# A hybrid encoder layer on one core: merges behind their accumulators' last additions, earlier block sums, combinations over more blocks

## The chip, the cores and the metric

The kernel runs as one program on one core of a Trainium2 chip. The metric is the device time of one launch in microseconds. The engines are named as in the profile: PE (TensorE, matrix products), DVE (VectorE), ACT (ScalarE), POOL (GpSimd) and SP (SyncE, which here issues most transfers). Each engine works through its own list of instructions in order and waits where an instruction needs the result of another engine or of a transfer.

## The reference

One layer of a streaming encoder for 2048 prompt tokens and 32 further tokens of a running stream, all in float32, with model width 1024 and a feed-forward width of 4096:

```
n = rmsnorm(x, g_mix);  z = n @ w_in
A = sliding-window attention with sinks (8 query heads, 2 key heads, width 64)
B = gated linear attention (4 heads, keys 64 wide, values 128), chunks of 64 tokens
h = x + concat(A, rmsnorm(B) * silu(rg)) @ w_out
y = h + relu(rmsnorm(h, g_ffn) @ w_up)^2 @ w_down
```

Beside y it returns the keys and values of the window and the state of the linear attention. The part that takes most of the time is the last line.

## The kernel before

A float32 product is done as three passes: each operand is split into a high part (rounded, a copy on ACT) and a low part (the rest, a subtraction on POOL or DVE), and PE sums high x high, high x low and low x high. `split_weight` and `weights` (the subtraction stands at L281 and L1454) do this for the weights, `load_tok` (L1578) for the tokens.

The program has four phases. Attention comes first, then linear attention (its decays E are formed on POOL at L946 and L954, and on DVE), then the output projection with the residual and the second norm (`op_phase`), then the feed-forward part.

**The feed-forward part** multiplies by Strassen's scheme in Winograd's form: seven products instead of eight. The tokens are in three environments, worked on in the order 1, 2, 0 with 356, 356 and 328 columns for a quarter. Each goes through 16 blocks of the feed-forward width (`NF`). A block has seven products with w_up (U) and seven with w_down (D); PE takes in turn the i-th of D for one block and the i-th of U for the block behind it, also across the border between environments. A product has twelve matmuls in two halves for each of two row groups, and for D each half has one PSUM tile of its own (`two`). DVE adds it from there to accumulators in SBUF, named P with the numbers 1 to 7 (L1580). At the end of an environment accumulators are added to one another on POOL (`merge`, L1679), and 2 to 5 are sent out (`store`, L1681). Merges with 7 and 1 are made in the last block but one. In the last block, product 1 is added to 6 and 2, and 5 and 7 to two accumulators each, so that only the merges of 6 into 3, 5 and 4 are left there.

**Weights.** The combinations of w_down's four quarters (S1 to S4) are formed ahead by `block_sums` (L723), four subtractions or additions on POOL for each part of a block, and stored in DRAM as `sd`: the first four blocks (EARLY) during attention, six more (MIDDLE) during linear attention, through one single buffer, the rest in the output projection. `down_sums` (L732) paces them: it runs beside the main text of a phase and yields numbers, which count PE time of the program's own running account until it is resumed: 6000 after a load, 3500 after each addition, 6000 after a store. In the first environment the split weights are also saved to DRAM (`save`, L1440) and read back by the others; those of the last block are made early by `keep_down`, one for each of blocks 2 to 8. `combine` (L1694) forms the token combinations of the last environment from quarters in DRAM: 8 pieces with four steps each (load, two subtractions, two more, store), one step with each product of D in blocks 9 to 13.

**The output projection** handles groups of columns; for a group it loads the residual (`load_y`, tile y), multiplies eight row pieces (PE, tile op), adds y on DVE (L1336), squares on ACT and accumulates on DVE (L1339); PE turns these into row sums (`oprb<-ones,acc`).

**What sets the order.** The text is run once by Python, and a scheduler sets each engine's list by its own running account of when operands will be ready and memory is free; loads on SP stand in the order in which it gets to them. An extra dependency without waiting (`after`) only orders two instructions. Memory that the sums' buffer takes in linear attention is used again by tiles of the projection, y among them.

Of the kernel before, what the change touches and what calls it, by code (L numbers as in the profile page):

```python
# [9 lines left out]
F32 = mybir.dt.float32  # L10
# [53 lines left out]
class Builder:  # L64
# [203 lines left out]
    def split_weight(self, src, hi, lo, hi_eng="act", lo_eng="pool", parts=1, after=None):  # L268
# [3 lines left out]
        for i in range(parts):  # L272
            ks = slice(i * k // parts, (i + 1) * k // parts)
            raw = tile_[:, ks]
            self.last_load = self.Q.dma_start(raw, src[:, ks]).ins
            if hi_eng == "act":
                self.after(self.S.activation(hi[:, ks], raw, AF.Copy), after)
            else:
                self.V.tensor_copy(hi[:, ks], raw)
            eng = self.G if lo_eng == "pool" else self.V  # L280
            eng.tensor_tensor(out=lo[:, ks], in0=raw, in1=hi[:, ks].bitcast(F32), op=ALU.subtract)  # L281

# [22 lines left out]
    def attention_phase(self):  # L305
# [3 lines left out]
        with ExitStack() as ctx:  # L309
# [337 lines left out]
            for i, t in enumerate(order):  # L647
# [13 lines left out]
                if i == 4:  # L661
                    early = [(b, c0, P) for b in range(EARLY) for c0 in range(0, 512, P)]
                    one = lambda name: self.mid.tile([P, 576], F32, tag="cc", name=name)
                    for j in range(2):
                        self.spawn(self.down_sums(early[j::2], one, 1, 3500), 13000 * j)
                if t == nt - 1:
# [64 lines left out]

    def down_sums(self, units, tile_, parts, step):  # L732

        for b, c0, n in units:
            raw = tile_(f"sd{b}_{c0}")[:, : 4 * n].rearrange("p (k m n) -> p k m n", k=2, m=2)
            self.load_block(raw, b, c0, n)
            yield 6000
            for _ in self.block_sums(raw, parts):
                yield step
            self.G.dma_start(self.sd[b][:, :, c0 : c0 + n], raw.rearrange("p k m n -> p (k m) n"))  # L740
            yield 6000

# [67 lines left out]
    def gla_phase(self):  # L810
        tc, a, V, S, G, Q = self.tc, self.a, self.V, self.S, self.G, self.Q
        nt = self.nt
        with ExitStack() as ctx:
# [274 lines left out]
            whole = lambda name: sums.tile([P, 2048], F32, tag="sd", name=name)  # L1088
            self.spawn(self.down_sums([(b, 0, 512) for b in range(EARLY, EARLY + MIDDLE)], whole, 2, 3500), 4000)
            for _ in gates(0):  # L1090
# [15 lines left out]
    def load_wout(self, pi, halves, engs):  # L1106
        w_out = self.a["w_out"].rearrange("(k p) n -> p k n", p=P)
        return [sum((self.wide_pairs(w_out, 512 * fh, f"wo{fh}", engs[j], (j,)) for j in range(2)), []) for fh in halves]

# [251 lines left out]
    def ffn_phase(self):  # L1361
# [4 lines left out]
        with ExitStack() as ctx:  # L1366
# [68 lines left out]

            products = lambda b: [DOWN[i] for i in (0, 4, 2, 1, 3, 5, 6)] if b == NF - 1 else DOWN
            kept, unsaved = self.kept, []

            def save():

                while unsaved:
                    key, t = unsaved.pop(0)
                    Q.dma_start(kept[key], f32(t))
# [86 lines left out]
            def down_weights(n, b, out):  # L1530
# [4 lines left out]
                for i, (x, _, _) in enumerate(products(b)):  # L1535
# [10 lines left out]
                    eng = V if n == 0 and i in (0, 5) and b < NF - 2 else G  # L1546
                    save()
                    out[x] = weights(f"d{b}{x}", None if made else src[x], g == 0, eng)
                    yield
                save()  # L1550

# [142 lines left out]
            def combine(step):  # L1694

                i = step % 4
                k, half = divmod(step // 4, 2)
                if k == H:
                    return
# [33 lines left out]
            for x, g, i in steps:  # L1733
# [6 lines left out]
                else:  # L1740
# [3 lines left out]
                    residual(g, i)  # L1744
                    if n == 0 and 2 <= b < 9 and i == 3:
                        keep_down(NF - 1, b - 2)
                    if n == 0 and 2 <= b < 9 and i == 5:
                        save()
                    if n == 0 and 9 <= b < 14:
                        combine(7 * (b - 9) + i)  # L1750
                    if b == NF - 2:
                        for q, x in {2: ((3, 5),), 3: ((5, 7), (4, 7)), 4: ((6, 1), (2, 1))}.get(i, ()):
                            merge(e, q, x)
                    if b == NF - 1 and i == 1:
                        for q in (3, 5, 4):
                            merge(e, q, 6)
                    if b == NF - 1 and i >= 3:
                        store(e, (3, 5, 2, 4)[i - 3], 1 + end)
                prepare()
# [142 lines left out]
```

## Time and profile before

| | us |
|---|---|
| three runs | 2267.05, 2274.03, 2277.59 (median 2274.03) |
| profiled execution | 2263.1, its span 2261.2 |
| PE busy in the span | 2142.3 (95%) |
| POOL busy | 1555.5 (69%) |
| DVE busy | 1545.1 (68%) |
| ACT busy | 1211.9 (54%) |

The span is what the hardware profiler saw of one execution, from the first to the last instruction; the execution's own time is 1.9 us longer. The median of the three runs is 10.9 us above that execution. Attention lasts until about 372 us, linear attention until about 715, the projection until about 903, and the feed-forward part until the end; the D products of its three environments end near 1390, 1848 and 2255. An idle stretch is given ahead of the instruction that ended it, with what released it; the row `<-issue` names nothing that the profile shows.

### The profile page before, as it was taken

Reading aid. Unit: us, or ns where it says so; the run is one execution under the profiler, and the core shown is the slowest. Engines: PE = TensorE matmul, PEld = TensorE weight load, DVE = VectorE, ACT = ScalarE, POOL = GpSimd, SP = SyncE. Lnnn points to the kernel's source line nnn. Section 1 sums busy time; section 2 is a strip of 40 time slices with the busy share of each in tenths; the row PEclk is TensorE's granted clock in tenths of the full one; section 3 lists DMA queues with packets and bytes.
Section 4 is the critical chain, followed back from the end, with each engine's and each line's share of the span. In section 5 each row is a group of like instructions: output and inputs, shape, how many; then the busy total and the mean of one; then the engine's idle time right before and its main releaser. Section 6 shows DMA issues by size and latency. Waiting matters only on the chain. (4 is left out here: it accounts for less than half of the span.)

```text
span 2261.2 us, 40634 instructions
## 1 busy us (share of the span) xinstructions
PE 2142.3 (95%) x14790; PEld 2010.9 (89%) x14790; DVE 1545.1 (68%) x3402; ACT 1211.9 (54%) x2692; POOL 1555.5 (69%) x1447
## 2 busy tenths in 40 slices
PE   7999999999987899999999997999999979999997
PEld 6777777888876899999999997999999979999996
DVE  7766766788993544677777764666666646766676
ACT  4555555656553122666665554566656636666662
POOL 4354555444446477778889896788877968888885
PEclk9999999999999899999999998999999989999998
DMA  7444564334345887644455575344444654444433
GB/s 249 149 154 135 199 211 141 136 110 157 101 158 180 337 332 289 232 148 156 163 180 179 164 274 180 125 139 136 136 138 130 246 198 138 143 154 143 152 112 113
DMA packets 191355, 391.00 MB, mean 173 GB/s; under 512 B 32417, under 2 KB 117586, under 8 KB 184242
## 3 DMA queue, kind: packets, MB, share of 16 engines
q1 hardware_dynamic: 157330, 331.36, 44.3%
q10 hardware_dynamic: 27120, 27.64, 3.5%
q0 software_dynamic: 6704, 29.40, 3.4%
q8 instruction: 117, 1.92, 0.3%
q14 instruction: 84, 0.69, 0.1%
HBM read 288.96 MB, written 99.38 MB: 172 GB/s over the span
## 5 line engine op out<-in xcount | busy, mean ns | idle before, releaser
L1580 DVE TENSOR_TENSOR P<-P,dn 128x712 f32<-128x712 f32 (+1 forms) x648 | 564.0, 875 | 271.2 <-PE dn L167 230.5
L44 ACT ACTIVATE u<-u 128x356 f32<-128x356 f32 (+1 forms) x384 | 174.2, 454 | 45.3 <-DVE u L1580 24.2
L44 ACT ACTIVATE r<-u 128x356 f32<-128x356 f32 (+1 forms) x192 | 88.5, 461 | 178.8 <-PE u L167 178.6
L1580 DVE TENSOR_TENSOR u<-u,r 128x356 f32<-128x356 f32 (+1 forms) x144 | 75.6, 525 | 105.9 <-PE u L167 88.0
L954 POOL TENSOR_TENSOR E<-cc 128x256 f32<-128x256 f32 (+1 forms) x117 | 68.5, 618 | 101.4 <-DVE cc L806 39.3
L1478 POOL TENSOR_TENSOR stage<-stage 128x512 f32<-128x512 f32 x90 | 116.6, 1295 | 16.5 <-DMA stage<-in_w_up 12.5
L723 POOL TENSOR_TENSOR sd<-sd 128x128 f32<-128x128 f32 (+2 forms) x136 | 101.0, 747 | 26.1 <-DMA sd<-in_w_down 21.6
L1030 DVE COPY_PREDICATED AT<-masks,A 64x64 f32<-64x64 int32 (+1 forms) x330 | 82.9, 253 | 23.0 <-ACT AT L44 12.3
L1580 DVE TENSOR_TENSOR uT<-u,uT 128x356 fp32r<-128x356 f32 (+1 forms) x192 | 94.2, 511 | 5.2 <-ACT uT L44 5.0
L1580 DVE TENSOR_TENSOR uB<-u,uB 128x356 fp32r<-128x356 f32 (+1 forms) x144 | 73.9, 513 | 26.3 <-ACT u L44 25.9
L44 ACT ACTIVATE uT<-u 128x356 fp32r<-128x356 f32 (+1 forms) x192 | 83.5, 457 | 7.7 <-DVE u L1580 7.1
L1336 DVE TENSOR_TENSOR y<-op,y 128x356 f32<-128x356 f32 (+1 forms) x48 | 23.9, 517 | 88.8 <-PE op L167 58.2
L1679 POOL TENSOR_TENSOR P<-P,P 128x712 f32<-128x712 f32 (+1 forms) x48 | 79.1, 1676 | 6.7 <-DVE P L1580 6.7
L44 ACT ACTIVATE P<-S,negm 128x192 f32<-128x192 f32 (+2 forms) x128 | 51.5, 417 | 45.1 <-DVE negm L588 31.1
L44 ACT ACTIVATE op<-y 128x356 f32<-128x356 f32 (+1 forms) x42 | 19.2, 467 | 93.0 <-DVE y L1336 89.3
L44 ACT ACTIVATE E<-E 128x1024 f32<-128x1024 f32 (+2 forms) x68 | 67.2, 1012 | 1.1
L44 ACT ACTIVATE uB<-u 128x356 fp32r<-128x356 f32 (+1 forms) x144 | 65.9, 457 | 3.0
L606 POOL TENSOR_TENSOR P<-P,es 128x512 f32<-128x512 f32 x15 | 15.5, 1034 | 68.8 <-ACT sq L44 27.1
L1580 DVE TENSOR_TENSOR u<-u,f 128x356 f32<-128x356 f32 (+1 forms) x96 | 49.9, 519 | 9.3 <-ACT u L44 9.3
L965 DVE TENSOR_TENSOR E<-E,kq 128x256 f32<-128x256 f32 (+1 forms) x117 | 54.2, 516 | 1.1 <-ACT E L44 1.0
L44 ACT ACTIVATE v<-go 128x256 f32<-128x256 f32 (+1 forms) x34 | 12.7, 379 | 75.5 <-DVE Sp L1062 39.4
L44 ACT ACTIVATE pS<-pT 128x256 f32<-128x256 f32 (+1 forms) x62 | 27.2, 491 | 43.2 <-PE pT L171 43.2
(1576 smaller groups left out, 8132.8 us busy)
## 6 DMA issues: line engine op xcount, KB each, us to landing
stage<-in_w_up SPq DMA_DIRECT2D x90, 512.0 KB, 4.0
stage<-sd SPq DMA_DIRECT2D x86, 512.0 KB, 4.7
stage<-in_w_down SPq DMA_DIRECT2D x43, 512.0 KB, 3.3
stage<-su SPq DMA_DIRECT2D x30, 512.0 KB, 4.1
sd<-sd POOLq DMA_DIRECT2D x12, 1024.0 KB, 5.5
stage<-in_w_down SPq DMA_DIRECT2D x46, 256.0 KB, 3.1
xT1a<-in_xT_prompt SPq DMA_DIRECT2D x16, 512.0 KB, 4.7
stage<-in_w_in SPq DMA_DIRECT2D x16, 512.0 KB, 5.5
```

What stands on the lines that cost most here:

```text
L44: ins = f(*args, **kw)
L606: (G if ch == 0 else V).tensor_tensor(out=dst, in0=src, in1=rb, op=ALU.mult)
L723: self.after(self.G.tensor_tensor(out=o, in0=x, in1=y, op=op), self.last_pe)
L954: G.tensor_tensor(out=e4, in0=c4, in1=ref, op=ALU.subtract)
L965: V.tensor_tensor(out=e4, in0=e4, in1=halves_of(kq, L, m), op=ALU.mult)
L1030: V.copy_predicated(dst, mk.unsqueeze(1).broadcast_to([L // nh, 2, w // m, m]), src[r].rearrange("s p (n m) -> s p n m", m=m),)
L1336: V.tensor_tensor(out=y[:, f], in0=ps, in1=y[:, f], op=ALU.add)
L1478: tt = lambda o, x, y, op: G.tensor_tensor(out=o, in0=x, in1=y, op=op)
L1580: add = lambda out, x, y, op=ALU.add: V.tensor_tensor(out=out, in0=x, in1=y, op=op)
L1679: G.tensor_tensor(out=e.acc[q][:, j : j + 2], in0=e.acc[q][:, j : j + 2], in1=e.acc[x][:, j : j + 2], op=ALU.add)
```

## The change

It has six parts.

1. `down_sums` takes its pauses as an argument. For EARLY nothing changes (3500 and 6000); for MIDDLE the step is 2200 and the pause 4000.
2. `split_weight` remembers its low part's instruction, and `load_wout` orders the high copies of the first output half's second part behind it.
3. The last block's D products run in the order 1, 6, 5, 3, 7, 4, 2; the last two were 2, 4.
4. The merges of 6 into 3, 5 and 4 were all given with product 6; now each is given with the product that adds last to that accumulator, and its store follows.
5. `save` may leave some weights unsaved for now: in the first environment saves lag two behind; in later blocks it isn't called here.
6. `keep_down` moves from blocks 2 to 8 to 7 to 13; `combine` takes four steps of every ten products, from block 2 to 13.

```diff
 def down_sums(self, units, tile_, parts, step, pause):
...
-            yield 6000
+            yield pause
...
-            self.spawn(self.down_sums([(b, 0, 512) for b in range(EARLY, EARLY + MIDDLE)], whole, 2, 3500), 4000)
+            self.spawn(self.down_sums([(b, 0, 512) for b in range(EARLY, EARLY + MIDDLE)], whole, 2, 2200, 4000), 4000)
...
-        return [sum((self.wide_pairs(w_out, 512 * fh, f"wo{fh}", engs[j], (j,)) for j in range(2)), []) for fh in halves]
+        part = lambda fh, j: self.wide_pairs(w_out, 512 * fh, f"wo{fh}", engs[j], (j,), self.last_low if j and not fh else None)
+        return [part(fh, 0) + part(fh, 1) for fh in halves]
...
-            products = lambda b: [DOWN[i] for i in (0, 4, 2, 1, 3, 5, 6)] if b == NF - 1 else DOWN
+            products = lambda b: [DOWN[i] for i in (0, 4, 2, 1, 3, 6, 5)] if b == NF - 1 else DOWN
...
-            def save():
+            def save(lag=0):
-                while unsaved:
+                while len(unsaved) > lag:
                     key, t = unsaved.pop(0)
...
-                    save()
+                    if g < 2:
+                        save(2 - 2 * g)
                     out[x] = weights(f"d{b}{x}", None if made else src[x], g == 0, eng)
                     yield
-                save()
...
-                i = step % 4
-                k, half = divmod(step // 4, 2)
-                if k == H:
+                i = step % 10
+                k, half = divmod(step // 10, 2)
+                if k >= H or i > 3:
                     return
...
-                    if n == 0 and 2 <= b < 9 and i == 3:
-                        keep_down(NF - 1, b - 2)
-                    if n == 0 and 2 <= b < 9 and i == 5:
+                    if n == 0 and 7 <= b < 14 and i == 3:
+                        keep_down(NF - 1, b - 7)
+                    if n == 0 and 7 <= b < 14 and i == 5:
                         save()
-                    if n == 0 and 9 <= b < 14:
-                        combine(7 * (b - 9) + i)
+                    if n == 0 and 2 <= b < 14:
+                        combine(7 * (b - 2) + i)
...
-                    if b == NF - 1 and i == 1:
-                        for q in (3, 5, 4):
+                    if b == NF - 1 and i >= 3:
+                        q = (3, 5, 4, 2)[i - 3]
+                        if q != 2:
                             merge(e, q, 6)
-                    if b == NF - 1 and i >= 3:
-                        store(e, (3, 5, 2, 4)[i - 3], 1 + end)
+                        store(e, q, 1 + end)
```

Two places show how instructions move. First SP, at the border of linear attention and the projection. `y00` and `y01` are the residuals of the first two groups, `u0raw` weights of the first U products, `mx0l` the third group's tokens, `sd10` a block to be summed. Before:

```order
L60 DMA u0raw_9185<-in_w_up 128x4x256 x2
L60 DMA mx0l_9162<-mix10_169 128x2848
L60 DMA ku0A11_9247<-u0A11_9244 128x1024
L60 DMA ku0A12_9251<-u0A12_9248 128x1024
L60 DMA sd10_9241<-in_w_down 128x1024 x2
L60 DMA y00_9180<-in_x_group0 128x2624
L60 DMA y01_9194<-in_x_group1 128x2624
```

And with the change:

```order
L60 DMA y00_9180<-in_x_group0 128x2624
L60 DMA u0raw_9185<-in_w_up 128x4x256 x2
L60 DMA y01_9194<-in_x_group1 128x2624
L60 DMA ku0A11_9247<-u0A11_9244 128x1024
L60 DMA ku0A12_9251<-u0A12_9248 128x1024
L60 DMA mx0l_9162<-mix10_169 128x2848
L60 DMA sd10_9241<-in_w_down 128x1024 x2
```

The first residual went from behind six loads and saves to the front, directly behind the last store of linear attention's state (`out_s_prompt`); the third group's tokens went behind the second residual and two saves.

Second POOL, at the end of the first environment. T4l is the low part of a token combination of the next environment, `stage` and `wf_u1...` its weights' combinations and splits for block 1, P3 to P6 the accumulators. Before:

```order
L1478 TENSOR_TENSOR stage_16139<-stage_16139,stage_16141 128x4x128
L1578 TENSOR_TENSOR T4l_10760<-T4l_10760,T4h_10759 128x712 x2
L1679 TENSOR_TENSOR P3_10749<-P3_10749,P6_10771 128x712
L1679 TENSOR_TENSOR P5_10750<-P5_10750,P6_10771 128x712
L1679 TENSOR_TENSOR P4_10773<-P4_10773,P6_10771 128x712
L1679 TENSOR_TENSOR P3_10749<-P3_10749,P6_10771 128x712
L1679 TENSOR_TENSOR P5_10750<-P5_10750,P6_10771 128x712
L1679 TENSOR_TENSOR P4_10773<-P4_10773,P6_10771 128x712
L1454 TENSOR_TENSOR wf_u1A11_15858<-stage_15854,wf_u1A11_15858 128x512
L1454 TENSOR_TENSOR wf_u1A12_15906<-stage_15856,wf_u1A12_15906 128x512
```

And with the change, whose lines are one further on here:

```order
L1479 TENSOR_TENSOR stage_16139<-stage_16139,stage_16141 128x4x128
L1579 TENSOR_TENSOR T4l_10760<-T4l_10760,T4h_10759 128x712 x2
L1680 TENSOR_TENSOR P3_10749<-P3_10749,P6_10771 128x712 x2
L1455 TENSOR_TENSOR wf_u1A11_15856<-stage_15852,wf_u1A11_15856 128x512
L1680 TENSOR_TENSOR P5_10750<-P5_10750,P6_10771 128x712 x2
L1455 TENSOR_TENSOR wf_u1A12_15906<-stage_15854,wf_u1A12_15906 128x512
L1680 TENSOR_TENSOR P4_10773<-P4_10773,P6_10771 128x712 x2
L1455 TENSOR_TENSOR wf_u1S2_15948<-stage_15904,wf_u1S2_15948 128x512
```

The six merges stood in one piece; they stand now in pairs, one accumulator at a time, with a split of a weight behind each pair.

More of the change, by code (lines that the diff above doesn't have):

```diff
@@ L280, in split_weight @@
             eng = self.G if lo_eng == "pool" else self.V
-            eng.tensor_tensor(out=lo[:, ks], in0=raw, in1=hi[:, ks].bitcast(F32), op=ALU.subtract)
+            self.last_low = eng.tensor_tensor(out=lo[:, ks], in0=raw, in1=hi[:, ks].bitcast(F32), op=ALU.subtract)
     def cols_pair(self, w, c0, name, engs=(("act", "pool"), ("act", "pool")), k0=0, nk=KB, after=None):
@@ L664, in attention_phase @@
                     for j in range(2):
-                        self.spawn(self.down_sums(early[j::2], one, 1, 3500), 13000 * j)
+                        self.spawn(self.down_sums(early[j::2], one, 1, 3500, 6000), 13000 * j)
                 if t == nt - 1:
@@ L730, in load_block, with down_sums @@
             self.after((queue or self.G).dma_start(raw[:, k], w[b, :, k, :, c0 : c0 + n]), self.last_pe)
-    def down_sums(self, units, tile_, parts, step):
+    def down_sums(self, units, tile_, parts, step, pause):
         for b, c0, n in units:
@@ L740, in down_sums @@
             self.G.dma_start(self.sd[b][:, :, c0 : c0 + n], raw.rearrange("p k m n -> p (k m) n"))
-            yield 6000
+            yield pause
     def prepare_gla(self, part):
```

## Prediction

> **What bounds the kernel now.** I read the header of the page first, then windows of 60 us, then every idle stretch of TensorE, and for the long ones the rows of the engines that released them.
>
> ```profile
> span 2261.2 us, 40634 instructions
> PE 2142.3 (95%) x14790; PEld 2010.9 (89%) x14790; DVE 1545.1 (68%) x3402; ACT 1211.9 (54%) x2692; POOL 1555.5 (69%) x1447
> PE   7999999999987899999999997999999979999997
> POOL 4354555444446477778889896788877968888885
> 720.00:780.00 60.00, 36.40 (x235) 36.13 (x234) 25.17 (x56) 10.90 (x24) 29.31 (x25) 0.80 0.85 314
> 780.00:840.00 60.00, 60.00 (x377) 60.00 (x376) 28.24 (x73) 12.13 (x22) 42.22 (x37) 1.00 0.88 338
> 1320.00:1380.00 60.00, 42.91 (x229) 41.65 (x228) 27.19 (x39) 22.93 (x45) 54.49 (x35) 0.83 0.66 239
> 1800.00:1860.00 60.00, 42.54 (x240) 41.32 (x240) 31.41 (x48) 21.51 (x48) 41.98 (x28) 0.83 0.67 235
> ```
>
> The columns of a window are its length, the busy time of PE, weight loads, DVE, ACT and POOL, then PE's clock, DMA's share and GB/s. TensorE is the bound: 2142.3 of 2261.2 us busy, and most windows, like 780 to 840, have no idle at all. Since no matmul is removed, the most that any change of order could win is what PE does not use: 118.9 us of idle, plus the time in which its clock was low. The idle is not spread out: three dips in the PE row of slices (one at the output projection, two at the ends of the first and second environment) hold 23.6 + 17.1 + 17.5 us, and the shares of POOL peak just before two of them.
>
> ```profile
> 745.37 1.27 PE L167 MATMUL oprb<-ones,acc 128*82 128x1 f32 x8 [23.60 <-DVE acc L1339]
> 1214.06 3.66 PE L167 MATMUL dn<-uT,wf_d10S 128*128 128x356 f32 x12 [3.12 <-DVE P L1580]
> 1369.71 2.12 PE L167 MATMUL dn<-uB,wf_d15S 128*128 128x356 f32 x6 [10.72 <-issue]
> 1374.72 2.12 PE L167 MATMUL dn<-uB,wf_d15S 128*128 128x356 f32 x6 [2.88 <-DVE P L1580]
> 1828.18 2.12 PE L167 MATMUL dn<-uB,wf_d15S 128*128 128x356 f32 x6 [10.88 <-issue]
> 1833.19 2.12 PE L167 MATMUL dn<-uB,wf_d15S 128*128 128x356 f32 x6 [2.89 <-DVE P L1580]
> 2240.49 1.33 PE L167 MATMUL dn<-uB,wf_d15S 128*128 128x328 f32 x6 [1.79 <-issue]
> 2245.13 1.98 PE L167 MATMUL dn<-uB,wf_d15S 128*128 128x328 f32 x6 [3.31 <-DVE P L1580]
> ```
>
> A row gives start, duration, the work, and in brackets how long the engine was idle ahead of it and for whom. These eight rows are the places that the change can reach; I take them in turn.
>
> **Output projection: the residual's load moves ahead.** The 23.60 us are a chain across four engines:
>
> ```profile
> 695.02 0.47 SPq L60 DMA_DIRECT2D out_s_prompt<-Sp  x1
> 719.93 0.58 POOL L740 DMA_DIRECT2D sd<-sd  x1
> 726.48 0.80 SPq L60 DMA_DIRECT2D y<-in_x_group  x2
> 732.60 3.38 DVE L1336 TENSOR_TENSOR y<-op,y 128x328 f32<-128x328 f32 x8 [29.77 <-DMA y<-in_x_group]
> 738.03 7.29 DVE L1339 TENSOR_TENSOR acc<-acc,op 128x328 f32<-128x328 f32 x7
> 714.29 0.42 PE L167 MATMUL op<-m1h,wo00h 128*128 128x328 f32 x1 [0.53 <-ACT op L44]
> y<-in_x_group SPq DMA_DIRECT2D x2, 1312.0 KB, 8.1
> 738.00:741.00 3.00, 0.00 (x0) 0.00 (x0) 2.86 (x6) 1.74 (x5) 1.74 (x2) 0.50 1.01 418
> ```
>
> POOL sends the last of the MIDDLE sums away at 719.93; only then is the space free into which SP loads the residual (726.48); it lands, DVE adds (732.60), accumulates (738.03), and PE can form the row sums at 745.37. The change's denser steps (2200 for 3500, pauses of 4000 for 6000) put that last store ahead of the last pieces of E, and SP's load right behind `out_s_prompt`, with no engine left to wait for. So it can be issued at about 695.5 and has landed by 695.5 + 8.1 = 703.6, before the products it is added to: those are all there when PE turns to the second half (714.29). DVE's eight additions and accumulations (3.38 + 7.29 for seven, so about 12 us) then run beside the products instead of behind them; the last sum comes some 2 to 3 us after 714.3 (an estimate: one of each, and ACT's square between), and PE, which reaches the row sums at 745.37 − 23.60 = 721.77, finds them there. The ceiling is 23.6 us and, by the clock of 0.50 in the last row, 1 more for the start behind it. The lower bound is DMA's: it is 0.85 and 0.88 busy in the two windows of this stage, so what PE no longer waits for may wait for transfers instead. The window with the stall moved 314 GB/s x 60 us = 18.8 MB; at the 338 of the next window that takes 55.7 us, a gain of 4.3. Against this, DMA reached 418 within the stall itself (738 to 741). Nearest is the ceiling, less a little for loads that come later: I take **22** (4 to 24.6).
>
> **Ends of the first two environments: merges behind the last additions.** Before, POOL adds acc6 into 3, 5 and 4 in one piece, ahead of the DVE additions to these:
>
> ```profile
> 1361.29 3.31 POOL L1578 TENSOR_TENSOR T4l<-T4l,T4h 128x712 fp32r<-128x712 f32 x2
> 1364.57 9.92 POOL L1679 TENSOR_TENSOR P<-P,P 128x712 f32<-128x712 f32 x6
> 1367.91 1.70 DVE L1580 TENSOR_TENSOR P<-P,dn 128x712 f32<-128x712 f32 x2 [9.89 <-POOL P L1679]
> 1374.00:1377.00 3.00, 2.28 (x8) 2.31 (x9) 0.70 (x2) 0.00 (x0) 0.49 (x1) 0.50 0.00 0
> 1379.09 2.11 PE L167 MATMUL dn<-uT,wf_d15S 128*128 128x356 f32 x12
> 1835.00:1838.00 3.00, 3.00 (x13) 3.00 (x12) 0.90 (x1) 0.00 (x0) 0.00 (x0) 0.50 0.53 155
> ```
>
> DVE stands 9.89 us for POOL; with one PSUM tile for each half, PE stands behind DVE: 10.72 us, and 2.88 once more two additions later. The change makes each merge follow its accumulator's last addition, so no addition waits for POOL. What goes: 10.72 + 2.88 = 13.6 at the first end and 10.88 + 2.89 = 13.8 at the second. To this comes the low clock: at 0.50 half of a busy time is lost, so 1.06 of the six matmuls' 2.12 at 1369.71, and 1.14 of the 2.28 busy in the window from 1374; at the second end 1.06 twice, and 1.50 of the 3.00 from 1835. Ceilings: 13.6 + 2.2 = 15.8 and 13.8 + 3.6 = 17.4. The six merges of 1.65 us are still to be done, between the splits of the next environment's weights. They may come from 1364.6 on, and the first split behind them is wanted when the three pairs of products that are left are through, some 12 us later (an estimate: six products of about 2.1 us, as at 1379.09); two merges (3.3) ahead of each split leave it room. SP's stores of the results wait for the merges, and loads queue behind them, but those are for later blocks. I take **15.5** (8 to 15.8) and **17** (9 to 17.4), the lower ends for half being given back to such a queue. The merges of block 14, ahead of these, stay where they were.
>
> **The last end.** Here the same six merges end the program:
>
> ```profile
> 2235.64 9.26 POOL L1679 TENSOR_TENSOR P<-P,P 128x656 f32<-128x656 f32 x6 [6.75 <-DVE P L1580]
> 2255.05 0.84 DVE L1580 TENSOR_TENSOR P<-P,dn 128x656 f32<-128x656 f32 x1 [0.35 <-PE dn L167]
> 2257.75 0.47 SPq L60 DMA_DIRECT2D out_yT_sample<-P  x1
> ```
>
> The waits of 1.79 and 3.31 us go, and the six matmuls behind the second need not take 1.98 (1.33 behind the first): 5.8. DVE is then the next limit (0.84 an addition, two to a product), so not all of it comes. The last accumulator, 2, needs no merge, and that of 4 (2 x 1.55) fits beside its additions; a merge that came last would cost 1.6 of the gain. I take **5.5** (3 to 5.8).
>
> **Middle of the first environment: combinations over twelve blocks, kept weights in 7 to 13.** The removed crowd is blocks 9 to 13:
>
> ```profile
> 1206.21 6.55 DVE L1454 TENSOR_TENSOR wf_d10A<-stage,wf_d10A 128x512 fp32r<-128x512 f32 x1
> L1454 DVE TENSOR_TENSOR wf_d10A<-stage,wf_d10A x2: 885/3716/6548, 1186.2 to 1206.2; 128x512 fp32r<-128x512 f32 x2
> L1454 DVE TENSOR_TENSOR wf_d4A<-stage,wf_d4A x2: 684/685/686, 1022.7 to 1039.6; 128x512 fp32r<-128x512 f32 x2
> 1165.00:1190.00 25.00, 24.38 (x150) 24.09 (x150) 18.61 (x28) 16.45 (x35) 23.08 (x22) 1.00 0.57 177
> L1710 POOL TENSOR_TENSOR quads<-quads x32: 487/566/1026, 1166.4 to 1272.6; 128x178 f32<-128x178 f32 x32
> ```
>
> The same split takes 0.685 us on DVE in block 4 and 6.55 in block 10, while POOL works without a gap; the addition queued behind it on DVE is late, and PE waits 3.12 us and then starts cold (12 matmuls in 3.66, in 2.11 at 1379.09): 4.7 us. The 32 combinations (0.566 us, 18 us together) are spread from 5 blocks to 12, so POOL's runs without a gap become shorter there, but blocks 2 to 8 get some that had none. I take **4** (−4.7, one such event more than now, to 4.7).
>
> In sentences of its own: the Trainium skill, "Advanced Engine Details and Errata", section "GPSIMD Details", says that POOL shares a read and a write interface with DVE and conflicts with DVE instructions that have two SBUF inputs, as this split has. The two rows above (0.685 and 6.55) agree. By that rule spreading combinations takes POOL's gaps from more DVE splits, which speaks against this part; it is the last rival below.
>
> **Denser sums, the second half of the output weights, saves two behind.** The sums' cost lies on POOL ahead of E:
>
> ```profile
> 485.54 2.38 POOL L954 TENSOR_TENSOR E<-cc 128x256 f32<-128x256 f32 x4 [24.90 <-PE A L167]
> 667.36 0.89 POOL L723 TENSOR_TENSOR sd<-sd 128x256 f32<-128x256 f32 x1 [8.99 <-DMA sd<-in_w_down]
> ```
>
> The same 48 additions are done, the last eight (8 x 0.89 = 7.1 us) ahead of E instead of behind, and POOL may stand for a load (8.99 here, of no harm at this place). POOL's idle ahead of E is up to 24.90 us and covers them; without it, the 7.1 would be PE's loss. I take **0** (−7 to 2). For the weights' second half the order of ACT's high copies is the same before and after, so **0**; saves two behind free SP for loads that PE does not wait for, **0** (−2 to 2).
>
> **Sum.** 22 + 15.5 + 17 + 5.5 + 4 = 64 us off the profiled execution's 2263.1: 2199. That execution is 10.9 us below the median of the runs shown, 2274.03, so the forecast is 2274.03 − 64 = **2210 us**. Bounds all at one end: 4 + 8 + 9 + 3 − 4.7 − 7 − 2 = 10.3 and 24.6 + 15.8 + 17.4 + 5.8 + 4.7 + 2 + 2 = 72.3; 2264 and 2202.
>
> **Rivals.**
>
> *DMA is the next bound in the projection.* For it: 0.85 and 0.88 busy in two windows running. Against: the 418 GB/s, and PE busy for all of the 60 us from 780. It gives 4.3 for 22: gain 46.3, **2228**.
>
> *POOL is the bound at the ends.* For it: POOL has 54.49 of 60 us in the window at 1320, and no gap ahead of the stall; merges that wait for DVE now stand ahead of the weight splits on an in-order engine, and each microsecond they wait is handed on. Against: at 1800 it has 41.98. If half of the 32.5 us comes back as waits for a split or a load: gain 47.8, **2226**.
>
> *The load is not free after all.* The order says what waits for which engine, not when; if the residual still lands late (its space given up by another tile, or POOL behind in the sums), the first term is nothing: gain 42, **2232**.
>
> *POOL without a gap slows DVE's splits through the first environment: slower.* One event cost 4.7 us. Blocks 2 to 13 have 24 of these splits. Without the 4 that I count, the other terms give 60; the change turns slower from 60 / 4.7 = 13 events on, over half of all. With 18: 84.6 − 60 = 24.6 lost, **2299**. For it: POOL is busy 23.08 of 25 us where combinations stand now. Against: with all of them packed into five blocks, one of the ten splits there was hit so hard.
>
> **Chances.** Forecast 0.60 (its own range 2199 to 2221), DMA 0.15, POOL at the ends 0.12, the load late 0.06, slower 0.04, and 0.03 that several small losses leave a change within 0.5% (11.4 us, about what can be told from none here). The first four are all faster: 0.93. To leave two in ten out, the range takes in the second to fourth case with some of their spread: 2196 to 2240.
>
> **What would show it.** In the profile after: no idle near 23 us ahead of `oprb`, and `y<-in_x_group` issued near 696; DVE additions at the ends without a wait for POOL's merges, PE's clock at 1.00 in windows like 1374 to 1377; merges in pairs, between splits; 5 to 6 us less from the last end's first wait (2238.70) to the end of the span; no DVE split above 2 us in blocks 2 to 13. PE's busy time stays near 2142 less the cold matmuls. Wrong would be new waits of PE for a weight split at either end, for `mx0l` or a weight in the projection, or for E in linear attention.

## The result, and the profile after

The changed kernel takes 2202.59 us (2198.86 to 2204.99) against 2275.81 for the kernel before: a ratio of 0.9683, 95% interval 0.9652 to 0.9714, so 73 us or 3.2% faster. The profiled execution took 2198.86 us, its span 2196.9.

First the header and the row of PE's slices of the page after, then four windows (columns as in the prediction):

```profile
span 2196.9 us, 40635 instructions
PE 2133.5 (97%) x14790; PEld 2002.9 (91%) x14790; DVE 1544.0 (70%) x3402; ACT 1212.9 (55%) x2692; POOL 1559.9 (71%) x1447
PE   7999999999999999999999999999999999999997
...
720.00:780.00 60.00, 60.00 (x390) 59.99 (x389) 27.52 (x68) 11.09 (x22) 38.05 (x34) 1.00 0.88 347
1300.00:1360.00 60.00, 53.08 (x307) 51.84 (x306) 38.51 (x58) 28.86 (x60) 55.56 (x36) 0.94 0.82 293
1322.00:1325.00 3.00, 2.05 (x7) 2.08 (x8) 0.81 (x2) 0.00 (x0) 3.00 (x2) 0.50 0.10 41
1337.00:1340.00 3.00, 3.00 (x21) 3.00 (x20) 2.57 (x4) 0.44 (x1) 3.00 (x3) 1.00 0.43 111
```

The three dips in PE's row are gone, and PE's busy time is 8.8 us shorter for the same 14790 matmuls, since fewer run at the low clock (granted clock 0.988 over the span, 0.975 before). PE is unused for 63.4 us of the span; before it was 118.9.

At the projection, the rows are SP's load of the first residual and DVE's first additions to it:

```profile
689.16 0.35 SPq L60 DMA_DIRECT2D y<-in_x_group  x1
697.95 2.14 DVE L1337 TENSOR_TENSOR y<-op,y 128x328 f32<-128x328 f32 x5 [2.17 <-DMA y<-in_x_group]
```

The load is issued at 689 instead of 726, DVE adds from 698, and PE has no wait ahead of its row sums. At the end of the first environment, POOL's merges and DVE's additions stand beside one another (POOL's rows first, then one of DVE and three of PE):

```profile
1336.53 3.43 POOL L1680 TENSOR_TENSOR P<-P,P 128x712 f32<-128x712 f32 x2
1339.93 1.28 POOL L1455 TENSOR_TENSOR wf_u1A<-stage,wf_u1A 128x512 fp32r<-128x512 f32 x1
1341.18 3.41 POOL L1680 TENSOR_TENSOR P<-P,P 128x712 f32<-128x712 f32 x2
...
1337.43 3.32 DVE L1581 TENSOR_TENSOR P<-P,dn 128x712 f32<-128x712 f32 x4 [2.05 <-PE dn L167]
...
1310.32 0.59 PE L167 MATMUL u<-T4h,wf_u15A 128*128 128x356 f32 x2 [1.66 <-POOL wf_u15A L1455]
1319.05 1.21 PE L167 MATMUL dn<-uT,wf_d15S 128*128 128x356 f32 x6 [1.69 <-DVE P L1581]
1322.95 2.12 PE L167 MATMUL dn<-uT,wf_d15S 128*128 128x356 f32 x6 [2.69 <-DVE P L1581]
```

DVE waits for PE now (2.05), no longer for POOL (9.89 before). What is left at this end are the waits at 1319 and 1323, behind the merges of block 14, which the change does not touch, and one at 1310 that is new: PE waits 1.66 us for the split of a weight on POOL. The prediction named such a wait as a sign of being wrong, and here it is small. It belongs to the sixth part: the profile with that part alone has 2.06 us there, while the kernel before and the three below without that part have none or 0.38.

To see where the time went, I compare the same matmuls in the two traces. Each line below is the time between two starts: the first `zk` of linear attention, its last `dk`, the first D matmul of block 1, 9 and 15 in the first environment, of block 1 in the second and third (and block 14, ahead of the second and third end), and the end of the span.

| stretch | before | after | difference |
|---|---|---|---|
| up to the first `zk` | 366.3 | 364.5 | −1.8 |
| linear attention (to the last `dk`) | 305.7 | 300.1 | −5.6 |
| projection and start of the feed-forward part | 278.5 | 257.5 | −21.0 |
| blocks 1 to 9 | 219.9 | 218.5 | −1.4 |
| blocks 9 to 15 | 170.1 | 171.4 | +1.3 |
| first end (block 15 to block 1 of the next) | 77.6 | 63.2 | −14.4 |
| second end (block 14 to block 1) | 101.9 | 85.1 | −16.8 |
| last end (block 14 to the end) | 58.1 | 53.5 | −4.6 |

Between the ends (block 1 to 14 of the second and third environment) nothing moved by more than 0.1. The differences add up to −64.3, what the two spans differ by. The starts that make up the first two lines are first and last numbers of these rows, of before and then of after:

```profile
L167 PE MATMUL zk<-nTb_0h,wkgh x16: 288/295/402, 366.3 to 376.5; 128*128 128x288 f32 x16
L167 PE MATMUL dk<-ones,qkp x132: 171/198/219, 386.6 to 672.0; 128*64 128x2 f32 x128, 128*32 128x2 f32 x4
```

```profile
L167 PE MATMUL zk<-nTb_0h,wkgh x16: 288/295/398, 364.5 to 374.7; 128*128 128x288 f32 x16
L167 PE MATMUL dk<-ones,qkp x132: 171/198/219, 384.9 to 664.6; 128*64 128x2 f32 x128, 128*32 128x2 f32 x4
```

In attention nothing was changed, and the other profiles have their first `zk` anywhere from 363.3 to 366.9. Two entries need an explanation: linear attention gained where the prediction had 0, and the third line is less than the stall of 23.6 and its cold start. From the last `dk` to the last row sums of the projection it is 239.6 before and 214.2 after, a gain of 25.4; from there to block 1 it is 38.9 and 43.3, a loss of 4.4. The rows of the changed kernel at this second place (PE's two waits, SP's load of the tokens T3, POOL's store of the last block sums):

```profile
882.79 0.43 PE L167 MATMUL u<-T3h,wf_u0S 128*128 128x356 f32 x1 [1.76 <-ACT T3h L44]
885.12 0.67 PE L167 MATMUL u<-T3l,wf_u0S 128*128 128x356 f32 x1 [1.91 <-POOL T3l L1579]
...
870.67 0.32 SPq L60 DMA_DIRECT2D T3l<-Td1T  x1
...
858.56 0.57 POOL L1319 DMA_DIRECT2D sd<-sd  x1 [0.30 <-POOL sd L723]
```

T3 was loaded at 866 before, 36.5 us ahead of the first U product at 902.5 (904.25 less its wait of 1.73); now it comes at 870.67, 1 us after the place of the first U product (871.41 less 1.73), behind a store of sums at 858.56 and, in SP's list, behind four loads of U weights (861.72 to 870.03). That the memory of the sums is what holds it back is tested below with seven blocks.

### The profile page after: what moved, and what is told of

Same layout as the page of the kernel before. It is cut to its first block, busy times and chain, and to the rows that moved or that the text cites. A ratio compares the mean times of both kernels' runs of the same rounds, so it can differ in the third digit from the quotient of the medians.

```text
span 2196.9 us, 40635 instructions
## 1 busy us (share of the span) xinstructions
PE 2133.5 (97%) x14790; PEld 2002.9 (91%) x14790; DVE 1544.0 (70%) x3402; ACT 1212.9 (55%) x2692; POOL 1559.9 (71%) x1447
## 4 chain that ended last, share of the span: by engine, by line
PE 53%; DMA 2%; POOL 1%; DVE 1%; ACT 1%; issue 1%; SPq 0%; POOLq 0%; ACTq 0%; DVEq 0%
PE dn L167 27%; PE u L167 26%; DVE P L1581 1%; DMA stage<-sd 0%; POOL P L1680 0%; DMA T3l<-Td0T 0%; DMA stage<-in_w_up 0%; DMA T2l<-Td0T 0%; DMA Td2T<-quads 0%; DMA quads<-Td2B 0%; POOL stage L1479 0%; DVE u L1581 0%; ACT uT L44 0%; DMA kd15S<-wf_d15S 0%; ACT u L44 0%
## 5 line engine op out<-in xcount | busy, mean ns | idle before, releaser
L1479 POOL TENSOR_TENSOR stage<-stage 128x512 f32<-128x512 f32 x90 | 117.1, 1301 | 17.3 <-DMA stage<-in_w_up 13.5
L1680 POOL TENSOR_TENSOR P<-P,P 128x712 f32<-128x712 f32 (+1 forms) x48 | 80.5, 1707 | 12.7 <-DVE P L1581 12.7
L1337 DVE TENSOR_TENSOR y<-op,y 128x356 f32<-128x356 f32 (+1 forms) x48 | 26.4, 563 | 66.0 <-PE op L167 63.2
L606 POOL TENSOR_TENSOR P<-P,es 128x512 f32<-128x512 f32 x15 | 15.5, 1034 | 68.9 <-ACT sq L44 27.2
L587 DVE TENSOR_REDUCE mx<-S 128x2 f32<-128x384 f32 (+2 forms) x64 | 32.8, 535 | 21.4 <-PE S L167 21.1
```

Of the source, the lines that this page charges most:

```text
L587: V.reduce_max(mx[:, ch, us], sp, axis=AX.X)
L606: (G if ch == 0 else V).tensor_tensor(out=dst, in0=src, in1=rb, op=ALU.mult)
L1337: V.tensor_tensor(out=y[:, f], in0=ps, in1=y[:, f], op=ALU.add)
L1479: tt = lambda o, x, y, op: G.tensor_tensor(out=o, in0=x, in1=y, op=op)
L1680: G.tensor_tensor(out=e.acc[q][:, j : j + 2], in0=e.acc[q][:, j : j + 2], in1=e.acc[x][:, j : j + 2], op=ALU.add)
```

## The experiments

The stretches named below are those of the table.

**The denser sums alone**, of all six parts:

```diff
-            yield 6000
+            yield pause
...
-... whole, 2, 3500), 4000)
+... whole, 2, 2200, 4000), 4000)
```

> The kernel before with only the denser pauses of the MIDDLE sums (2200 and 4000). My theory: these alone free the residual's memory in time, so the 23.6 us of idle ahead of the first row sums go, and with them the stretched DVE instructions at the tail of linear attention (some 5 us); of this about 4 us are given back at the start of the feed-forward part, since token loads stand behind others there. So 26 us faster (ratio 0.9885). Rival 1 (the load of the residual needs the other reordered parts too): the idle stays, under 8 us faster. Rival 2 (the give-back comes from another part): 30 us or more faster, without new waits on T3h and T3l.

Measured: 2245.18 us, ratio 0.9871 (0.9854 to 0.9887), 28.5 us faster. Linear attention 301.4, projection and start 257.5, as in the changed kernel; from the last row sums to block 1 43.4. So these two numbers alone free the residual's memory, shorten linear attention, and cost the 4.4 us at the start of the feed-forward part; the first rival (other parts needed) and the second (the loss from elsewhere) are out.

**The merges alone**, with the new order of the last block's products:

```diff
-            products = ... (0, 4, 2, 1, 3, 5, 6) ...
+            products = ... (0, 4, 2, 1, 3, 6, 5) ...
...
-                    if b == NF - 1 and i == 1:
-                        for q in (3, 5, 4):
+                    if b == NF - 1 and i >= 3:
+                        q = (3, 5, 4, 2)[i - 3]
+                        if q != 2:
                             merge(e, q, 6)
```

> The kernel before with only the order 1, 6, 5, 3, 7, 4, 2 in the last block and each merge of 6 behind the accumulator's last addition. My theory: the three ends give 14.4 + 16.8 + 4.6 = 36 us, as between the profiles of before and after (ratio 0.984). Rival (POOL is the bound at the first end, and what the combinations' move freed on POOL is needed): the first end gives half, so 29 us or less (ratio 0.987).

Measured: 2239.85 us, ratio 0.9845 (0.9820 to 0.9871), 33.8 us faster with an interval of 29 to 41. The ends take 61.4, 84.2 and 53.2: 16.2, 17.7 and 4.9 less than before. POOL, though it has no gap there, does not take the gain back.

**The combinations and kept weights alone**, and then **everything but them**:

```diff
-                i = step % 4
+                i = step % 10
...
-                    if n == 0 and 2 <= b < 9 and i == 3:
+                    if n == 0 and 7 <= b < 14 and i == 3:
...
-                    if n == 0 and 9 <= b < 14:
+                    if n == 0 and 2 <= b < 14:
```

> The kernel before with only keep_down in blocks 7 to 13 and combine over blocks 2 to 13. Prediction on record: 4 us faster, since no DVE split is stretched to 6.55 us any more (ratio 0.998). Rival (the time between the first D of block 1 and of block 15 differs by 0.1 us between before and after, so what the middle gains is lost again nearer to the end, where keep_down now stands): within 2 us of before, with new waits after block 9 or so.

> The changed kernel with combine and keep_down where they were before. If the part is worth nothing, as the landmarks of the two profiles say: 73 us faster than before within 2 us, like the changed kernel (ratio 0.968). If the part is worth its 4 us and another part took them back: 4 us slower than the changed kernel (ratio 0.970). If it costs: faster than the changed kernel.

Measured: alone 2268.67 us, ratio 0.9979 (0.9965 to 0.9994), 5 us faster. Without them 2205.99 us, ratio 0.9691 (0.9663 to 0.9719), which cannot be told from the changed kernel's 0.9683. The landmarks of single executions had misled me: in the profile without this part, blocks 9 to 15 take 178.1 us, and the reason is the one the prediction named. The groups of DVE's splits, first without the part, then with it (shortest, median and longest in ns):

```profile
L1455 DVE TENSOR_TENSOR wf_d9A<-stage,wf_d9A x2: 1384/4189/6994, 1130.4 to 1148.4; 128x512 fp32r<-128x512 f32 x2
L1455 DVE TENSOR_TENSOR wf_d10A<-stage,wf_d10A x2: 1633/3544/5455, 1161.3 to 1181.1; 128x512 fp32r<-128x512 f32 x2
L1455 DVE TENSOR_TENSOR wf_d11A<-stage,wf_d11A x2: 1504/3949/6394, 1191.0 to 1210.8; 128x512 fp32r<-128x512 f32 x2
...
1156.73 3.57 PE L167 MATMUL dn<-uT,wf_d9S 128*128 128x356 f32 x11 [3.59 <-DVE P L1581]
```

```profile
L1455 DVE TENSOR_TENSOR wf_d10A<-stage,wf_d10A x2: 1402/1524/1645, 1158.4 to 1179.2; 128x512 fp32r<-128x512 f32 x2
```

Three splits of 5.5 to 7.0 us in this execution, one of 6.5 in that of before; with the sums alone there are three (5.0 to 7.0), with the merges alone one (7.0). Where the combinations are spread, eight of ten profiles have none above 1.95, those of the part alone and of the changed kernel among them; the low parts on DVE (below) have one of 4.60, the later merges at the first end one of 6.45. So spreading makes these events rarer and does not exclude them. Blocks 9 to 15 take 177.3 and 178.1 us in the two profiles with three events, 170.1 and 171.9 in the two crowded ones with one, 170.9 to 173.5 where the combinations are spread: three events cost some 6 us, while a single one does not show in this stretch.

Alone, the three gains add up to 67.3 us (28.5, 33.8 and 5.0) against the 73 of all six parts, which the intervals of the three allow.

**The changed kernel again**, as the measure for three further kernels:

> The changed kernel once more, as the measure for the three that follow: 2202 us within 4 (ratio to before 0.968).

Measured: 2200.06 us, ratio 0.9678 (0.9663 to 0.9692).

**Pauses halfway between**, to separate a late store from work beside DVE:

```diff
-... whole, 2, 2200, 4000), 4000)
+... whole, 2, 2850, 5000), 4000)
```

> The changed kernel with pauses halfway for the MIDDLE sums (2850 and 5000). In the profiles a unit takes 38.6 us with the change and 58.8 before; halfway it should take about 49, so the sixth ends near 670 us, still ahead of the residual's load (689), but its last additions run beside DVE's splits of m0l and wo00l at the tail of linear attention. My theory (two effects: a late store, which only counts past 689, and DVE instructions stretched beside POOL's additions): no idle ahead of the first row sums, and linear attention (first zk to last dk) 303 to 312 us in place of 300, so 3 to 10 us slower than the changed kernel. Rival (the gain in linear attention comes from something else in the denser sums, such as E coming earlier): linear attention stays at 300 to 301, no slower than 1 us.

Measured: 2209.60 us, ratio 0.9722 (0.9705 to 0.9739), 9.5 us slower than the changed kernel. The last of the sums is sent off at 662.5, well ahead of the residual's load, and the projection stays short (no idle ahead of the row sums); linear attention takes 306.9. Near its end DVE multiplies E beside POOL's sums, and then beside POOL's split of the second output weights, which stands directly behind them (POOL's rows second). The last fence has the later three instructions in the changed kernel, where POOL has neither beside them:

```profile
652.05 2.72 DVE L965 TENSOR_TENSOR E<-E,kq 128x256 f32<-128x256 f32 x3
656.17 5.48 DVE L965 TENSOR_TENSOR E<-E,kq 128x256 f32<-128x256 f32 x3
...
651.81 4.45 POOL L723 TENSOR_TENSOR sd<-sd 128x256 f32<-128x256 f32 x5
656.22 5.09 POOL L281 TENSOR_TENSOR wo01l<-stage,wo01h 128x1024 fp32r<-128x1024 f32 x2
```

```profile
647.39 1.16 DVE L965 TENSOR_TENSOR E<-E,kq 128x256 f32<-128x256 f32 x3
```

A product takes 0.91 us beside the sums and 1.83 beside the split, instead of 0.39. The end is only half of the loss, though: 3.5 of the 6.8 us between the two kernels are there before the last but one `dk`. At 515.19 PE waits 2.53 us for DVE, as it does not in the changed kernel, and behind that wait its clock is 0.50 (from 518 to 521), so that such a wait costs more than its length. So the denser sums have two effects: the last store comes ahead of the residual's load, and other DVE instructions stand beside POOL's work.

**Seven blocks' sums in linear attention**, five in the projection:

```diff
-EARLY, MIDDLE = 4, 6
+EARLY, MIDDLE = 4, 7
...
-        when = (..., (0, 24, 28, 30), (2, 29, 32, 34))
+        when = (..., (0, 24, 28, 30))
```

> The changed kernel with seven blocks' sums in linear attention, not six, and five in the projection, the one that came last there left out. On SP the loads of T3, B22 and T4 then stand ahead of the weights of the first U products. My theory (the 4.4 us lost at the start of the feed-forward part are the tokens that wait for the store of the projection's last sum): from the last row sums to the first D of block 1 39 us in place of 43.3, and 4 us faster in all, if the seventh sum, which ends near 645, does not stretch DVE at the tail of linear attention (then 2 to 8 us of it are lost again). Rival (transfers as such are the bound there): 43 us stay.

Measured: 2201.28 us, ratio 0.9681 (0.9667 to 0.9695), no different from the changed kernel. T3 is loaded at 842.75, ahead of the first U product, and the waits for its parts are gone, but PE waits further on for ACT, and linear attention takes 302.3:

```profile
883.00 0.40 PE L167 MATMUL u<-T2h,wf_u0S 128*128 128x356 f32 x1 [2.70 <-ACT u L44]
```

From the last row sums to block 1 it is 37.3 us, less than the 39 expected, but the row sums themselves come 6.1 us later behind the last `dk`; projection and start together take 257.6, as in the changed kernel. From the first U product to block 1 it is 48.7 us, with 50.7 in the changed kernel and 46.3 before. So the tokens' load behind the last block's sums is the cause of 2 of the 4.4 us; what holds the rest is open, and the 2 are lost again ahead of the first U product.

**The low parts of the second output weights on DVE**, not POOL:

```diff
-self.load_wout(0, (0,), [(("act", "dve"),) * 2, (("act", "pool"),) * 2])
+self.load_wout(0, (0,), [(("act", "dve"),) * 2] * 2)
```

> The changed kernel with the low parts of wo01 on DVE too, not on POOL. In the changed kernel's profile DVE needs 3.35 and 3.32 us for the low parts of wo00 while POOL makes those of wo01 (6.17), and 1.21 each before the change, when POOL had no such work beside them. My theory (POOL's work beside DVE's stretches it): four splits of 1.2 on DVE, 4.8 in place of 6.7, and the wait of 4.22 for DVE shrinks to about 2: 2 us faster in linear attention. Rival (each split takes what it takes, 3.3): 13 us on DVE and 6 us slower.

Measured: 2200.92 us, ratio 0.9680 (0.9665 to 0.9694), no difference. First the changed kernel's DVE, then this one's, and one wait of its PE:

```profile
648.87 3.36 DVE L281 TENSOR_TENSOR wo00l<-stage,wo00h 128x1024 fp32r<-128x1024 f32 x1
```

```profile
651.36 1.21 DVE L281 TENSOR_TENSOR wo00l<-stage,wo00h 128x1024 fp32r<-128x1024 f32 x1
...
661.65 3.19 PE L167 MATMUL A<-E 64*64 64x64 f32 x102 [2.54 <-DVE g L1074]
```

The mechanism is as expected (1.21 with POOL idle, 3.36 beside its splits), the price is not: DVE is through with four splits in less time than with two (4.9 us, not 6.7), but PE's wait of 4.22 becomes three of 1.94, 0.89 and 2.54.

**Without the order of the high copies, and with every save at once**:

```diff
-        part = lambda fh, j: self.wide_pairs(..., self.last_low if j and not fh else None)
+        (as before the change)
...
-                    if g < 2:
-                        save(2 - 2 * g)
+                    save()
...
+                save()
```

> The changed kernel without the order of the second half's high copies and with every save at once, as before. Prediction on record: both are worth nothing (0, and -2 to 2): 2201 us within 3 (ratio to before 0.968). Rival (saves that lag keep SP free for loads in the first environment, which the prediction counted as nothing): 4 us or more slower than the changed kernel, lost between the first D of block 1 and block 9.

Measured: 2202.58 us, ratio 0.9688 (0.9674 to 0.9703). Within what can be told, the two together are worth nothing.

**Denser still, with seven blocks**:

```diff
-... whole, 2, 2200, 4000), 4000)
+... whole, 2, 1800, 3200), 4000)
```

(and the two lines for seven blocks above.)

> The changed kernel with seven blocks' sums in linear attention at pauses of 1800 and 3200, so that the seventh ends near 600 us, as the sixth does in the changed kernel, ahead of the tail's DVE splits. My theory: linear attention 300 us again (302.3 with seven at the pauses of the change), the start of the feed-forward part 2 us shorter as there: 2 to 3 us faster than the changed kernel (ratio 0.967). Rival (denser still puts POOL's additions ahead of E, or stretches DVE earlier): linear attention 303 us or more, slower than the changed kernel.

Measured: 2206.67 us, ratio 0.9711 (0.9696 to 0.9725), slower than the changed kernel by some 5 us. In the profiled execution, the slowest of the four (2210.17), projection and start take 253.2 us, 4.3 less than in the changed kernel, but linear attention takes 313.0, with two waits for DVE that are new:

```profile
512.48 0.41 PE L171 MATMUL dk<-packed,E 128*128 128x128 f32 x2 [2.85 <-DVE AT L977]
592.29 0.66 PE L171 MATMUL dk<-packed,E 128*128 128x128 f32 x2 [3.67 <-DVE AT L977]
```

My theory fell here: it is not only the tail, whose wait of 4.2 us is the same in both kernels. How dense the sums are decides which DVE instructions they fall beside, and of the settings tried 2200 and 4000 is the best, not one step on a slope.

**Two more merges moved behind additions**, of accumulator 1 into 6 and 2:

```diff
-                        for q, x in {2: ((3, 5),), 3: ((5, 7), (4, 7)), 4: ((6, 1), (2, 1))}.get(i, ()):
+                        for q, x in {2: ((3, 5),), 3: ((5, 7), (4, 7))}.get(i, ()):
                             merge(e, q, x)
+                    if b == NF - 1 and i == 1:
+                        for q in (6, 2):
+                            merge(e, q, 1)
```

> The changed kernel with its own rule applied to two more merges: accumulator 1 is added to 6 and 2 only after the last block's second product, not in the block before. In the changed kernel's profile PE still waits for DVE additions behind such merges: 0.88, 1.69 and 2.69 us at the first end, 2.88, 0.81 and 0.29 at the second, 1.05 at the third, 10.3 in all, with some cold matmuls behind. My theory (an addition behind a merge on POOL is the cause): these go, 6 to 10 us faster than the changed kernel (ratio 0.964 to 0.966). Rival (POOL is full there, and the same 6.7 us of merges delay the splits of the tokens or weights of the next environment): within 2 us, with new waits for T or a weight at the first end.

Measured: 2204.99 us, ratio 0.9700 (0.9684 to 0.9716), about 5 us slower. From the first D of block 14 to block 1 behind the first end it is 87.2 us instead of 92.4, as hoped; but the second end takes 92.4 instead of 85.1. The rows are one of POOL, one of DVE and one of PE there:

```profile
1788.34 6.85 POOL L1680 TENSOR_TENSOR P<-P,P 128x712 f32<-128x712 f32 x4
...
1800.54 1.59 DVE L1675 COPY P<-dn 128x656 f32<-128x656 f32 x2 [1.53 <-DMA out_yT_prompt<-P]
...
1801.49 3.40 PE L167 MATMUL dn<-uT,wf_d0S 128*128 128x328 f32 x12 [5.16 <-issue]
```

POOL's merges end at 1795, the stores that need them go out behind, and the next environment's first copies into the same accumulators wait for the stores: PE stands 5.16 us. That is the rival of the prediction in which POOL bounds the ends; the change meets it only in the 1.66 us at 1310, and 6.7 us of merges more reach it.

**The same at the first end only**:

```diff
-4: ((6, 1), (2, 1))}.get(i, ()):
+4: ((6, 1), (2, 1)) if n else ()}.get(i, ()):
                             merge(e, q, x)
+                    if n == 0 and b == NF - 1 and i == 1:
```

> The changed kernel with the later merges of accumulator 1 at the end of the first environment only. With them at all ends the second end lost 7.3 us, since the next environment's first copies into accumulators waited for stores that the merges had made late (DVE's copy idle for the store at 1800.54), while the way from the first D of block 14 to the second environment's block 1 was 5.2 us shorter (87.2 us in place of 92.4). My theory: 5 us faster than the changed kernel, 2196 us (ratio 0.966). Rival (POOL's later work at the first end is lost again in block 0 behind it, as the wait of 1.70 us at 1354 suggests): 2200 us or more.

Measured: 2198.08 us, ratio 0.9674 (0.9653 to 0.9694). The way from block 14 over the first end is 89.1 us, 3.3 less than in the changed kernel. By the ratios it is 1 to 2 us faster than the changed kernel (0.9678 and 0.9683), and the intervals overlap: that it is any faster is not shown.

## Why the prediction was right, and where it was not

The forecast was 2210 us with a range of 2196 to 2240; measured were 2202.59. The spans differ by 64.3 us, and the sum was 64, but that is partly luck: the terms that it counted brought 56.9, linear attention, which it put at nothing, 5.6, and attention, where nothing was changed, 1.8. Between the medians it is 73 us, more than the 72.3 that all terms at their best would give.

- **The projection, 22.** The stall of 23.6 went as described, to the step: the store out of the way, the load at 689 instead of 695.5, DVE beside the products. The gain is 25.4 there. The rival (a bound by transfers) held at one place in a milder form: 4.4 us come back at the start of the feed-forward part, 2 of them because the tokens' load stands behind the last sums; the other 2.4 stay open. Net 21.0.
- **The ends, 15.5, 17 and 5.5.** 14.4, 16.8 and 4.6 in the changed kernel, 16.2, 17.7 and 4.9 with the merges alone, the first two a little over the ceilings of 15.8 and 17.4. The cold clock was worth counting: without it they would have been put at 13.6 and 13.8.
- **The middle, 4.** Right in size (5 us alone, interval 1.4 to 8). In mechanism it holds for the number of events, fewer where the combinations are spread, but not for the price of 4.7 us that was put on one: before and after, blocks 1 to 15 differ by 0.1 us, though the profile of before has one event and that of the changed kernel none. The spread kernel has waits of its own there, among them the 1.66 us for POOL at 1310.
- **Denser sums, 0.** This is the step that failed. The prediction put the sums' cost "on POOL ahead of E", and covered it by POOL's idle time. It lies on DVE beside POOL, where the term was 0 (−7 to 2) and 5.6 us and more were gained: with the old pauses linear attention took 305.7, 313.6 and 313.3 us (before, merges alone, combinations alone, whose instructions stand in the same order there), with the new ones and six blocks 299.4 to 301.6. The Trainium skill, "Advanced Engine Details and Errata", section "GPSIMD Details", says that POOL shares a read and a write interface with DVE and conflicts with DVE instructions that have two SBUF inputs. The runs agree: the products of E took 0.39 us with POOL idle, 0.91 beside the sums and 1.83 beside the split of the weights, the splits on DVE 1.21 and 3.36. The prediction applied that rule to the combinations and not to the sums, whose neighbours (the products E with kq, the splits of the output weights) are just such instructions. How much of the gain comes from the sums themselves and how much from the split that stands behind them on POOL was not separated.
- **From the profiled execution to the median.** The forecast put both kernels the same 10.9 us above their profiled executions. That of before lay 12.7 us below the median of the four runs, that of the changed kernel 3.7 below its own: hence 73 us between the medians with 64 between the profiles. Linear attention may be a part of it (305.7 us in the profile of before, 313.6 and 313.3 in the two others with that part unchanged), but this is not shown: the merges alone were profiled 7.9 us below their median with the 313.6.

The slower rival needed 13 costly splits in blocks 2 to 13; with the combinations spread there were none above 2 us in eight profiles and one in each of two.

## What to carry to other kernels

Where an accumulator is merged on one engine and added to on another, put the merge behind the last addition: the same instructions, 34 us less here. Then ask who needs the merged value's memory next, because that sets how late a merge may be (5.16 us lost where it was too late). And when work is moved in time on POOL, look at what DVE does beside it at the new and the old place, not only at what stands behind it on POOL.

## What the runs showed of the hardware

A DVE subtraction with both inputs in SBUF took 0.685 us at its quickest and up to 6.99 beside a busy POOL; DVE's additions with one input in PSUM took 0.85 to 0.90 a piece in the same stretches (1.70 for two at 1367.91 in the profile of before). The long ones end when POOL pauses. In the profile of before the split that starts at 1206.21 and takes 6.55 us ends at 1212.76, 0.55 us after the first of these two rows of POOL, which has a gap of 3.31 between them:

```profile
1210.92 1.29 POOL L1454 TENSOR_TENSOR wf_u11S<-stage,wf_u11S 128x512 fp32r<-128x512 f32 x1
1215.52 1.29 POOL L1454 TENSOR_TENSOR wf_d10A<-stage,wf_d10A 128x512 fp32r<-128x512 f32 x1 [3.31 <-ACT wf_d10A L44]
```

So it lay beside five further instructions of POOL and ended only behind the last of them. The split of 6.99 us in the kernel without spread combinations and that of 6.45 with the later merges at the first end also end 0.54 to 0.55 us behind POOL's last instruction before a gap. I had expected such splits to be rare. Linear attention, where DVE has instructions of this kind beside POOL's sums, differs by 5.6 to 13.5 us between the old and the new setting of the sums and by 7.9 between executions with the same order of instructions (305.7 and 313.6); in the slower one seven products of E take 4.13 us beside the sums, 2.51 in the other, and PE then waits 3.67 us for DVE.

And PE's granted clock fell to 0.50 behind waits as short as 1.69 and 2.69 us close together, with 1.21 us of work between them (the window from 1322 above), not only behind those of 10 us.
